# Blocks of two experts with four contraction rows instead of four experts with two, in a two-block transformer kernel on one Trainium2 core

## The chip, the core and the metric

The kernel runs on one core of a Trainium2 chip. A core has a matrix engine (PE, whose weight loads the profile lists apart as PEld), a vector engine (DVE), a scalar engine (ACT), a general engine (POOL) and an engine that here only issues transfers (SP). They run side by side, each through its own list of instructions in a fixed order, and wait for each other through semaphores. Weights come from the chip's memory (HBM) in transfers that 16 engines carry out. PE writes its results to PSUM, eight banks of 512 floats on each of 128 partitions; everything else is in SBUF. The metric is the time of one execution on the device, in microseconds (us).

## The reference

Two transformer blocks over 256 tokens of width 1024. The first mixes two kinds of attention and then sends each token to two of 32 experts; the second attends over the tokens and a context and has a plain gated MLP. The change lies in the first block's experts:

```python
def hierarchical_moe(h, w_group, w_router, w_gate, w_up, w_down):
    group_logits = jnp.einsum('td,dg->tg', h, w_group)      # top-1 of 4 groups
    ...
    top_p, top_i = lax.top_k(in_prob, EXPERT_TOPK)          # top-2 of its 8 experts
    ...
    for grp in range(N_GROUPS):
        hid = (jax.nn.silu(jnp.einsum('td,edf->tef', h, w_gate[grp]))
               * jnp.einsum('td,edf->tef', h, w_up[grp])) * combine[:, grp, :, None]
        y = y + jnp.einsum('tef,efd->td', hid, w_down[grp])
    return y
```

An expert's gate and up matrices are 1024 x 256, its down matrix 256 x 1024, all float32: 1 MB each, 96 MB for the 32 experts.

## The kernel before

The 32 experts are worked off in eight units of four (the loop over `u`). An expert has 32 places for tokens, so a unit has 128. For a unit, `gather(u)` makes the rows of its places, transposed, by products of x with one-hots (`pgat`, two groups of 16 instructions, each group followed by DVE's `xg`). Gate and up products (`pgu`) put four experts side by side on four groups of 32 columns of PE, eight contraction steps k each. ACT takes the silu (`sg`), DVE multiplies by the other half, PE transposes (`pth`), ACT copies (`hid`). The down products (`pyd`) fill two PSUM banks, one for each half nh of the 1024 columns, in two contraction steps k2. Each half is copied as a high part by ACT (`yh`) and a low part by DVE (`yl`), and products with transposed one-hots (`pst`, `ST`) scatter both into four running sums (`acc`, two token tiles by two halves).

The weights come in blocks of 1 MB, `[128, 2048]` floats, twelve for a unit: four each of gate (`eg`), up (`eu`) and down (`ed`). `wexp` makes one with a single transfer, issued by SP in `load_block` (L164). The blocks rotate through 21 slots (14 from unit 4 on); SP waits for the slot's last reader, then issues. Gate and up contraction row d sits on partition p = d // 8 with k = d % 8, so a partition's eight rows of an expert are 8 KB in a row in memory. A quarter took two of the eight rows, for all four experts: runs of 2 KB. A down block took one of a partition's two rows and one half of its columns, for four experts: also 2 KB.

```python
src = src.rearrange("e (p k) c -> p e (k c)", k=8)[:, :, part * 512:part * 512 + 512]
```

Between units 3 and 4 lies a branch (L1200) for tokens beyond an expert's 32 places, which all engines take part in; with these inputs it is not entered. From unit 5 on, PE also works on the context of block 2: the transposes of the normed context (`pt`, from `cx`), the projections `ckap`, `ckbp`, `cvbp`, and the transposes of its heads (`pka`, `pqk`). In unit 7 the sums are added to `x` (L1344), scaled to `xf` (L1348) and squared by ACT (`jk`, L1350), for each half and token tile; the sums of squares (`ss`) and then the splits of block 2's first weights (`lkah`, `lkal`) stand behind that.

The order on each engine isn't the order of the code: a scheduler sets it when the kernel is built, from its own estimates, save for a few pairs fixed by `after`. So a change in one place can move instructions elsewhere. On PE the helper records all products at L99 and all transposes at L102.

Of the kernel before, what the change touches and what calls it, by code (L numbers as in the profile page):

```python
# [22 lines left out]
# columns of the shape-only constant array  # L23
C_ID, C_TRI = 0, 128
C_IO = 256                     # 1..32 along the free axis
C_DN = C_IO + 32               # 8..1
C_SP = C_DN + 8                # p % 32 + 1
C_BM = C_SP + 1                # [p, 4]: p // 32 == j
C_SL = C_BM + 4                # rows of a modulation chunk's partial sums: latent, context
C_LT = C_SL + 2                # [i, j] of 8 by 8: j < i  # L30
C_W = C_LT + 64
# columns of the one of block 2's attention
C_ROPE = 0                     # [p, 2 token tiles, cos 64 | signed sin 64]
C_CM = C_ROPE + 256            # [p, 64]: NEG where the column lies outside row 63 - p % 64's neighbourhood
C_J = C_CM + 64                # reversal of each half's 64 rows, times the root of the head's size
# [3 lines left out]
def constants():  # L39
    """arrays that depend on the shapes alone"""  # L40
# [31 lines left out]
    # [e, unit, slot]: e == 4 * unit + slot // 32  # L72
# [4 lines left out]
class Ordered:  # L77
    """the tensor engine; between start() and stop() it takes its instructions in the program's order"""
# [16 lines left out]
    def stop(self):  # L95
        self.on = False
# [9 lines left out]
def tile_kernel(ctx: ExitStack, tc: tile.TileContext, I, out, dbg=None):  # L106
# [9 lines left out]
    def open_stage(name, psum, base=False):  # L116
        """the pools of one stage; psum: banks per tag"""
# [14 lines left out]
    def open_part(name, psum):  # L132
        """pools of a part of the stage: SBUF for what only the part needs, and all of its PSUM"""
        st = ExitStack()
        S_["tmp"] = st.enter_context(tc.tile_pool(name="tmp_" + name, bufs=1, reuse_waits="tile"))
        S_["ps"] = st.enter_context(tc.tile_pool(name="ps_" + name, bufs=1, space=PSUM, reuse_waits="tile"))
        S_["banks"] = psum
        return st
# [17 lines left out]
    # ---------------------------------------------------------------- helpers  # L156
    def load_block(src, name, extra=None):
        """src: DRAM AP [128, a, b] with a * b = 2048; extra: a pool and its slots that the stage adds to the ring"""
# [8 lines left out]
    def cols(w, c0, n=256):  # L167
        """columns c0:c0+n of a [1024, *] matrix, contraction row d = p * 8 + k"""
        return w[:, c0:c0 + n].rearrange("(p k) c -> p k c", k=8)

    def rows(w, r0):
        """rows r0:r0+256 of a [*, 1024] matrix, contraction row k * 128 + p"""
# [28 lines left out]
    def after(ins, first):  # L201
        """ins behind first in their engine's order"""
# [6 lines left out]
    def bcast_dma(dst, src, n):  # L209
        """n elements of DRAM copied to all partitions"""  # L210
        SP.dma_start(dst, bass.AP(tensor=src.tensor, offset=src.offset, ap=[[0, P], [1, n]]))

    def rstd_of(ssq, n, mean, eps, name):
        """(ssq * mean + eps) ** -0.5 over [128, n]"""
# [6 lines left out]
    def row_ssq(src, name, col=None):  # L221
        """src [128, 2, 1024] -> sums of squares [128, 2]"""
# [9 lines left out]
    def row_rstd(src, name):  # L232
        """src [128, 2, 1024] -> rstd [128, 2]"""
        return rstd_of(row_ssq(src, name), 2, 1.0 / D, EPS, name)

    def diags(r, name):
        """diagonal matrices of the two columns of r [128, 2]"""
# [5 lines left out]
    def norm_rows(src, name):  # L243
        """the rows' rstd, a column for each token tile"""
# [3 lines left out]
    def pairs_T(src, dg, tags, by_pair=False):  # L248
        """four PSUM tiles of pairs of k, [128 d, 2, 256 t]: see scaled_T"""
# [10 lines left out]
    def scaled_T(src, dg, tags, by_pair=False):  # L260
        """yields k, PSUM [128 d, 256 t] of src[t, p * 8 + k], times r[t] where dg = diags(r);
        tags: the banks of the four pairs of k, each open until its pair was taken"""
# [3 lines left out]
    # -------------------------------------------------------------- constants  # L266
# [13 lines left out]
    cols_ = const.tile([P, 4, 8], F32)    # gains down the partitions: attn_norm, ffn_norm, norm1_g, norm2_g  # L280
    gA, gF, gN1, gN2 = (cols_[:, i] for i in range(4))
    lvl = ab([P, 5, 32], "lvl", "lvl", dt=BF16)     # masks of the doubling

    mqk = ring.tile([P, 2048], F32, tag="blk", name="mqk")
    POOL.memset(mqk[:, :P], 0.0)                 # takes its slot of the ring
# [21 lines left out]
    maskn = const.tile([P, P], BF16)      # [j, i]: NEG where j > i  # L307
    maskc = const.tile([P, P], BF16)      # [i, j]: NEG where j > i

    # ============================================================ block 1: norm  # L310
# [33 lines left out]
    PE.transpose(pm, tri, ident)          # [i, j]: j <= i  # L344
# [15 lines left out]
    # ------------------------------------------------- modulations of block 2  # L360
# [4 lines left out]
    DVE.tensor_tensor(sc2t, sc2t, c2t, op=ALU.mult)                         # silu  # L365
    sil = ep.tile([P, 8, 2, 16], F32, tag="sil", name="sil")
    POOL.tensor_copy(sil, bc(sc2t.rearrange("p a k -> p k a"), 16))
    mod = pers.tile([P, 6, 8, 2], F32, tag="mod", name="mod")     # [p, vector, k, latent / context], d = p * 8 + k
    w_mod = I["w_mod_2"][0]

    def mod_steps():
        """a vector's quarters by column groups: column 8 c + k of group j is d = (32 j + c) * 8 + k, and blocks of 32
        by 32, transposed, bring its two sides to mod's places"""
# [35 lines left out]
    # ------------------------------------------------------ GDN q, k, v with conv  # L409
    gT = {}  # L410

    def proj_T(c0, name, sink):
        """columns c0:c0+256 in two [128 ch, 256 t] PSUM tiles, each given to sink with its place; a step at a time"""
# [21 lines left out]
    def gdn_proj(kind, base):  # L435
        def conv(c, pp_):
# [11 lines left out]
            DVE.scalar_tensor_tensor(o, th, 1.0, a, op0=ALU.add, op1=ALU.mult)   # 2 * silu  # L448
# [17 lines left out]
    # ------------------------------------------------------------- gates  # L466
# [1361 lines left out]
```

## Time and profile before

| What | Value |
|---|---|
| median of 3 runs | 882.71 us (881.35 to 885.22) |
| profiled execution, span | 879.8 us |
| PE busy | 825.3 us, 94% of the span |
| DVE, ACT, POOL busy | 422.3, 296.3, 105.6 us |
| transfers | 200.18 MB, mean 228 GB/s |
| eg, eu, ed blocks | 32 each, 1024 KB, 14.1 us median from issue to landing |

The span runs from the first to the last instruction that the profiler saw; the time of a run also holds what lies before and after. The experts run from about 228 to 477 us of the span. Busy shares are means over stages with different limits, so the stretches below say more than the table. A row of a timeline merges neighbours of the same kind on an engine: start, length, engine, line, operation, result <- operands, shapes, count, and in brackets how long the engine had been idle before and what ended that.

### The profile page before, as it was taken

How to read it: one execution, taken by the hardware profiler on the slowest of the kernel's cores; microseconds unless marked ns; L12 is line 12 of the kernel's file. 1: busy time of each engine (PE TensorE's matmuls, PEld its weight loads, DVE VectorE, ACT ScalarE, POOL GpSimd, SP SyncE). 2: the span in 40 equal slices, each digit the busy share in tenths (PEclk: the TensorE clock that was granted, in tenths of full speed). 3: DMA queues.
4: the chain of work that ended last, by engine and by line, in shares of the span. 5: the costliest groups of instructions: out<-in, count | busy, mean ns of one | idle time of the engine just before them, and what ended most of it. 6: DMA issues, size and time to landing. Idle time of an engine off the chain costs nothing.

```text
span 879.8 us, 15327 instructions
## 1 busy us (share of the span) xinstructions
PE 825.3 (94%) x6436; PEld 667.5 (76%) x6436; DVE 422.3 (48%) x927; ACT 296.3 (34%) x523; POOL 105.6 (12%) x90
## 2 busy tenths in 40 slices
PE   9999999999789988996998997999997999999997
PEld 8887887867656645773865897667686999999996
DVE  4866454644322111323224788555664655545555
ACT  4542143433110000101004662456643444444332
POOL 3111000332000000000000577100022100000000
PEclk9999999999889999897999999589999999999999
DMA  7999787495799999999599135010271655555101
GB/s 218 353 386 391 264 296 281 133 385 171 280 386 386 387 387 387 378 382 376 208 386 333 48 53 164 1 48 2 96 239 48 202 187 187 192 191 187 54 1 48
DMA packets 123416, 200.18 MB, mean 228 GB/s; under 512 B 15481, under 2 KB 62001, under 8 KB 123345
## 3 DMA queue, kind: packets, MB, share of 16 engines
q1 hardware_dynamic: 123152, 199.08, 64.5%
q8 instruction: 51, 0.84, 0.4%
q0 software_dynamic: 192, 0.11, 0.1%
q14 instruction: 21, 0.16, 0.1%
HBM read 198.23 MB, written 1.05 MB: 226 GB/s over the span
## 4 chain that ended last, share of the span: by engine, by line
PE 47%; DVE 4%; POOL 4%; issue 3%; DMA 2%; ACT 1%; SPq 1%; DVEq 0%; POOLq 0%; ACTq 0%
PE pfg L99 7%; PE pfu L99 7%; PE pf L99 7%; PE sc L99 6%; PE pgat L99 3%; PE pgu L99 2%; PE po L99 2%; PE ptp L102 2%; POOL latl L192 2%; PE pyd L99 2%; DMA eg<-in_w_gate_dram 1%; PE ckbp L99 1%; PE pqa L99 1%; PE pqb L99 1%; POOL rq L218 1%
## 5 line engine op out<-in xcount | busy, mean ns | idle before, releaser
L99 PEld LDWEIGHTS pgat<-S,x 128*128 128x128 f32 x256 | 62.5, 335 | 3.7 <-DVE xg L1051 2.1
L99 PE MATMUL pgat<-S,x 128*128 128x128 f32 x256 | 63.0, 404 | 0.6 <-PEq L1200 0.5
L99 PE MATMUL pfu<-lof,fuh 128*128 128x256 f32 x176 | 50.2, 285 | 0.0
L99 PE MATMUL pfu<-hif,fuh 128*128 128x256 f32 x176 | 50.2, 285 | 0.0
L99 PE MATMUL pfu<-hif,ful 128*128 128x256 f32 x176 | 50.2, 285 | 0.0
L99 PE MATMUL pfg<-hif,fgl 128*128 128x256 f32 x160 | 45.3, 283 | 0.0
L99 PE MATMUL pfg<-lof,fgh 128*128 128x256 f32 x160 | 45.2, 283 | 0.0
L99 PE MATMUL pfg<-hif,fgh 128*128 128x256 f32 x160 | 45.2, 283 | 0.0
L192 DVE TENSOR_TENSOR fdl<-fd,fdh 128x512 fp32r<-128x512 f32 x44 | 27.5, 687 | 31.0 <-ACT fdh L185 31.0
L1051 DVE TENSOR_TENSOR xg<-pgat,cols__83 128x512 f32<-128x512 f32 x15 | 10.4, 692 | 63.7 <-PE pgat L99 63.7
L99 PE MATMUL pyd<-ed,hid 128*32 128x512 f32 x256 | 34.1, 664 | 3.8 <-ACT hid L1326 3.8
L1320 ACT ACTIVATE sg<-pgu,r1s 128x256 f32<-128x256 f32 x8 | 3.8, 474 | 96.7 <-PE pgu L99 73.9
L1545 DVE TENSOR_REDUCE st<-sc 128x1 f32<-128x512 f32 x32 | 21.9, 691 | 28.6 <-PE sc L99 28.3
L185 ACT ACTIVATE fdh<-fd 128x1024 fp32r<-128x1024 f32 x22 | 22.1, 1052 | 39.0 <-issue 39.0
L99 PE MATMUL pf<-fdl,fh 128*128 128x512 f32 x88 | 35.0, 398 | 0.0
L99 PE MATMUL pf<-fdh,fh 128*128 128x512 f32 x88 | 34.7, 394 | 0.0
L99 PE MATMUL pf<-fdh,fl 128*128 128x512 f32 x88 | 34.1, 393 | 0.0
L99 PEld LDWEIGHTS pfu<-hif,fuh 128*128 128x128 f32 x176 | 34.1, 194 | 0.0
L99 PEld LDWEIGHTS pfu<-hif,ful 128*128 128x128 f32 x176 | 34.1, 193 | 0.0
L99 PEld LDWEIGHTS pfu<-lof,fuh 128*128 128x128 f32 x176 | 34.0, 193 | 0.0
L185 ACT ACTIVATE fuh<-fu 128x1024 fp32r<-128x1024 f32 x22 | 22.1, 1052 | 31.2 <-issue 28.7
L99 PE MATMUL sc<-k,qa 128*128 128x256 f32 (+1 forms) x64 | 28.1, 501 | 3.7 <-DVE qa L1149 3.5
(691 smaller groups left out, 2209.6 us busy)
## 6 DMA issues: line engine op xcount, KB each, us to landing
eg<-in_w_gate_dram SPq DMA_DIRECT2D x32, 1024.0 KB, 14.1
eu<-in_w_up_dram SPq DMA_DIRECT2D x32, 1024.0 KB, 14.1
ed<-in_w_down_dram SPq DMA_DIRECT2D x32, 1024.0 KB, 14.1
wmod<-in_w_mod_dram SPq DMA_DIRECT2D x24, 1024.0 KB, 9.5
fg<-in_w_gate_dram SPq DMA_DIRECT2D x11, 1024.0 KB, 5.4
fu<-in_w_up_dram SPq DMA_DIRECT2D x11, 1024.0 KB, 5.3
fd<-in_w_down_dram SPq DMA_DIRECT2D x11, 1024.0 KB, 5.0
kv<-in_w_in_dram SPq DMA_DIRECT2D x5, 1024.0 KB, 13.9
```

Source lines behind the costliest of these rows:

```text
L99: return self._keep(self.engine.matmul(*args, **kwargs))
L102: return self._keep(self.engine.transpose(*args, **kwargs))
L185: S_["hi"] = ACT.activation(hf[:, s], vf[:, s], AF.Copy)
L192: i = (POOL if c in pool else DVE).tensor_tensor(lf[:, s], vf[:, s], hf[:, s], op=ALU.subtract)
L218: S_["pow"] = POOL.tensor_tensor(r, v, mhalf[:, :n], op=ALU.pow)
L1051: DVE.tensor_tensor(xg[:, ks], p, bc(gF[:, ks], P), op=ALU.mult)
L1320: ACT.activation(sg, pgu[:, 0], AF.Silu, scale=r1s[:, u:u + 1])
L1545: DVE.tensor_reduce(t_[:, 0, s_:s_ + 1], sc, axis=AX.XY, op=ALU.max)
```

## The change

A block now holds two experts instead of four, and for each a run of 4 KB: four of a partition's eight gate or up rows, or a whole row of the down matrix. `part % 2` chooses the pair of experts, `part // 2` the half of the contraction rows. Each step k of a gate or up product thus reads two blocks (j = 0, 1 from one, j = 2, 3 from the other). Since a down block now has all columns of one contraction row, the loop over k2 goes outside that over the halves, both banks are open at once, and both copies come behind all 32 instructions. The line that kept unit 7's second half behind the scatter of the first is gone.

```diff
-        src = w[u // 2, 4 * (u % 2):4 * (u % 2) + 4]
-        if name == "ed":
-            src = src.rearrange("e (p k) c -> p e k c", k=2)[:, :, part % 2, part // 2 * 512:part // 2 * 512 + 512]
-        else:
-            src = src.rearrange("e (p k) c -> p e (k c)", k=8)[:, :, part * 512:part * 512 + 512]
-        return load_block(src, name, extra)
+        e0 = 4 * (u % 2) + 2 * (part % 2)
+        src = w[u // 2, e0:e0 + 2].rearrange("e (p k) c -> p e (k c)", p=P)
+        return load_block(src[:, :, part // 2 * 1024:part // 2 * 1024 + 1024], name, extra)
...
-                                     rhs=ww[k // 2][:, j, k % 2 * 256:k % 2 * 256 + 256], start=k == 0, stop=k == 7)
+                                     rhs=ww[k // 4 * 2 + j // 2][:, j % 2, k % 4 * 256:k % 4 * 256 + 256], start=k == 0, stop=k == 7)
...
-        for nh in range(2):
-            py = pt_([P, 512], ("y", "y" if u < IFU else "cx")[nh], "pyd")
-            for k2 in range(2):
+        pys = [pt_([P, 512], t, "pyd") for t in ("y", "y" if u < IFU else "cx")]
+        for k2 in range(2):
+            for nh, py in enumerate(pys):
                 for j in range(4):
-                    m = PE.matmul(py[32 * j:32 * j + 32], lhsT=hid[:, k2, 32 * j:32 * j + 32],
-                                  rhs=dw[2 * nh + k2][:, j], start=k2 == 0, stop=k2 == 1)
-                    if u == 7 and nh and j + k2 == 0:
-                        after(m, S_["sc"])
+                    PE.matmul(py[32 * j:32 * j + 32], lhsT=hid[:, k2, 32 * j:32 * j + 32],
+                              rhs=dw[2 * k2 + j // 2][:, j % 2, nh * 512:nh * 512 + 512], start=k2 == 0, stop=k2 == 1)
+        for nh, py in enumerate(pys):
             yh = c2.tile([P, 512], F32R, tag="y", name="yh", bufs=NY)
```

The order of the transfers on SP stays as it was, and so does that on POOL. Units 0 to 2 keep their order on PE. What moves on PE, in unit 3 behind the transposes of the hidden rows (acc_2743 and acc_2745 are the sums of the first half of the columns, acc_2744 and acc_2746 those of the second; an order row of `pyd` or `pgu` counts one for two instructions of the trace):

```order
-L99 MATMUL pyd<-ed,hid 32x512 x8
+L99 MATMUL pyd<-ed,hid 32x512 x16
 L99 MATMUL acc_2743<-yh,ST 128x512
 L99 MATMUL acc_2745<-yh,ST 128x512
-L99 MATMUL pyd<-ed,hid 32x512 x4
+L99 MATMUL acc_2744<-yh,ST 128x512
+L99 MATMUL acc_2746<-yh,ST 128x512
 L99 MATMUL acc_2743<-yl,ST 128x512
 L99 MATMUL acc_2745<-yl,ST 128x512
-L99 MATMUL pyd<-ed,hid 32x512 x4
-L99 MATMUL acc_2744<-yh,ST 128x512
-L99 MATMUL acc_2746<-yh,ST 128x512
```

The down products were cut in three with the first half's scatter between them; now they stand in one row, with all scatter products behind.

PE in unit 4, from the scatter on (pgat is the gather for unit 5, in two groups):

```order
+L99 MATMUL acc_2744<-yh,ST 128x512
+L99 MATMUL acc_2746<-yh,ST 128x512
 L99 MATMUL acc_2743<-yl,ST 128x512
 L99 MATMUL acc_2745<-yl,ST 128x512
 L99 MATMUL pgat<-S,x 128x128 x8
-L99 MATMUL pyd<-ed,hid 32x512 x4
-L99 MATMUL pgat<-S,x 128x128 x8
-L99 MATMUL acc_2744<-yh,ST 128x512
-L99 MATMUL acc_2746<-yh,ST 128x512
 L99 MATMUL acc_2744<-yl,ST 128x512
 L99 MATMUL acc_2746<-yl,ST 128x512
+L99 MATMUL pgat<-S,x 128x128 x8
```

Between the two groups of the gather stood the last quarter of the down products; now one pair of scatter products stands there. Unit 6 moves in the same way. In unit 5, behind the context's projection `ckbp`, 16 rows of up products stand instead of 8, and 8 fewer ahead of it.

DVE at the end of unit 7, before:

```order
L1338 TENSOR_TENSOR yl<-pyd,yh 128x512
L1344 TENSOR_TENSOR x<-x,acc_2743 128x512
L1344 TENSOR_TENSOR x<-x,acc_2745 128x512
L1348 TENSOR_TENSOR xf<-x,fB 128x512 x2
L1338 TENSOR_TENSOR yl<-pyd,yh 128x512
L1344 TENSOR_TENSOR x<-x,acc_2744 128x512
L1344 TENSOR_TENSOR x<-x,acc_2746 128x512
```

And the same place now (the lines of the code are four fewer):

```order
L1334 TENSOR_TENSOR yl<-pyd,yh 128x512 x2
L1340 TENSOR_TENSOR x<-x,acc_2743 128x512
L1340 TENSOR_TENSOR x<-x,acc_2745 128x512
L1340 TENSOR_TENSOR x<-x,acc_2744 128x512
L1340 TENSOR_TENSOR x<-x,acc_2746 128x512
L1344 TENSOR_TENSOR xf<-x,fB 128x512 x4
```

All four additions now stand ahead of the first scaling. ACT's eight squarings keep their order, x and xf in turn.

## Rows read from the trace of the kernel before

**Rows 1.** Stretches: length, busy us (count) by engine, clock, transfer share, GB/s

```profile
80.00:88.00 8.00, 7.89 (x74) 7.07 (x72) 4.33 (x13) 1.45 (x2) 3.01 (x4) 1.00 1.03 410
...
287.00:309.40 22.40, 20.82 (x204) 14.43 (x203) 3.73 (x6) 2.05 (x4) 0.00 (x0) 1.00 1.05 386
...
400.00:410.00 10.00, 5.91 (x29) 1.41 (x27) 2.93 (x6) 2.35 (x4) 0.00 (x0) 0.53 1.05 369
```

**Rows 2.** Timeline of SP, the loads of block 2's modulation

```profile
70.53 25.07 SPq L164 DMA_DIRECT2D wmod<-in_w_mod_dram  x6
```

**Rows 3.** Waits of PE, 225 to 490 us: us in total, times, longest

```profile
PE pth L102 <- DVE sg L1321: 7.3, 6, 1.9
...
PE pth L102 <- DMA eg<-in_w_gate_dram: 0.6, 1, 0.6
...
PE pgc L102 <- DVE gcol L1280: 0.3, 1, 0.3
PE pst L99 <- DVE gcol L1280: 0.2, 1, 0.2
```

**Rows 4.** Timeline of PE and ACT, down products of units 2 and 3

```profile
296.15 3.64 PE L99 MATMUL pyd<-ed,hid 128*32 128x512 f32 x32 [0.47 <-ACT hid L1326]
...
299.86 0.60 ACT L1337 ACTIVATE yh<-pyd 128x512 fp32r<-128x512 f32 x1 [1.06 <-PE pyd L99]
...
318.61 1.92 PE L99 MATMUL pyd<-ed,hid 128*32 128x512 f32 x16 [0.47 <-ACT hid L1326]
...
326.08 0.73 PE L99 MATMUL acc<-yl,ST 128*128 128x512 f32 x2
```

**Rows 5.** Timeline, unit 4's last up products and its silu

```profile
343.59 3.66 PE L99 MATMUL pgu<-eu,xg 128*32 128x256 f32 x64
...
348.07 0.47 ACT L1320 ACTIVATE sg<-pgu,r1s 128x256 f32<-128x256 f32 x1 [22.77 <-SPq L1200]
```

**Rows 6.** Timeline of PE and DVE, the gathers in units 4 and 6

```profile
350.15 2.78 PE L99 MATMUL pyd<-ed,hid 128*32 128x512 f32 x24 [0.53 <-ACT hid L1326]
...
354.15 3.85 PE L99 MATMUL pgat<-S,x 128*128 128x128 f32 x16
...
358.93 4.10 PE L99 MATMUL pgat<-S,x 128*128 128x128 f32 x16
...
366.96 4.18 PE L99 MATMUL pt<-dgc,cx 128*128 128x128 f32 x16 [1.14 <-issue]
...
445.79 3.64 PE L99 MATMUL pyd<-ed,hid 128*32 128x512 f32 x32 [0.47 <-ACT hid L1326]
...
454.49 0.69 DVE L1051 TENSOR_TENSOR xg<-pgat,cols__83 128x512 f32<-128x512 f32 x1 [3.42 <-PE pgat L99]
...
454.76 0.62 PE L99 MATMUL acc<-yl,ST 128*128 128x512 f32 x2
455.24 4.10 PE L99 MATMUL pgat<-S,x 128*128 128x128 f32 x16
```

**Rows 7.** Timeline of PE, unit 5 around the context's heads

```profile
395.02 1.07 PE L99 MATMUL pgu<-eu,xg 128*32 128x256 f32 x16
399.23 1.09 PE L102 MATMUL pqk<-cst,qn__3722 128*128 128x128 f32 x4 [3.14 <-DVE qn__3722 L1089]
...
405.50 4.69 PE L99 MATMUL pyd<-ed,hid 128*32 128x512 f32 x24 [0.47 <-ACT hid L1326]
```

**Rows 8.** Timeline of PE, DVE and ACT, end of unit 7

```profile
468.47 1.92 PE L99 MATMUL pyd<-ed,hid 128*32 128x512 f32 x16 [0.47 <-ACT hid L1326]
...
472.38 1.29 DVE L1344 TENSOR_TENSOR x<-x,acc 128x512 f32<-128x512 f32 x2 [0.59 <-PE acc L99]
...
474.36 0.63 ACT L1350 ACTIVATE jk<-xf 128x512 bf16<-128x512 f32 x1 [0.54 <-DVE xf L1348]
...
479.62 0.63 ACT L1350 ACTIVATE jk<-x 128x512 bf16<-128x512 f32 x1
...
480.37 0.63 ACT L1350 ACTIVATE jk<-xf 128x512 bf16<-128x512 f32 x1
```

More of the change, by code (lines that the diff above doesn't have):

```diff
@@ L1340, in tile_kernel @@
                 PE.matmul(acc[2 * tt + nh], lhsT=ST[:, tt * P:(tt + 1) * P], rhs=yh, start=u == 0, stop=False)
-                S_["sc"] = PE.matmul(acc[2 * tt + nh], lhsT=ST[:, tt * P:(tt + 1) * P], rhs=yl, start=False, stop=u == 7)
+                PE.matmul(acc[2 * tt + nh], lhsT=ST[:, tt * P:(tt + 1) * P], rhs=yl, start=False, stop=u == 7)
                 if u == 7:
```

## Prediction

> **What bounds the kernel now.** I read the trace in this order: busy time by stretch, the waits of PE, then the timelines of the places where the change moves something.
>
> By stretch first. While the experts run, the transfer engines are full: from 287 to 309 us they move 386 GB/s at a share of 1.05 [rows 1]. One block of 1,048,576 bytes takes 2.72 us at that rate. If this set the pace, longer runs would be the thing to want. PE, however, is busy 20.82 of the 22.40 us of that stretch [rows 1], and the list of what PE waited for between 225 and 490 us has one row with a transfer in it, 0.6 us [rows 3]; even there the same place also hangs on the heads of the context. PE's larger waits are short handovers to DVE and ACT: 7.3 us in six pieces before the transposes of the hidden rows [rows 3]. So the blocks arrive ahead of their use, and the stage is PE's instruction stream plus the handovers in it. A faster load is worth something only where somebody waits for its landing.
>
> There is one such place. In unit 4 PE's last up product ends at 347.25 (343.59 + 3.66), but ACT's silu starts at 348.07, and what released it is SP behind the branch on overflow [rows 5]. SP leaves that branch when the loads that it had issued have landed, so this release hangs on the transfers.
>
> **The change part by part.**
>
> *The loads.* As many blocks, as many bytes, half as many runs, twice as long. The trace of before holds runs of 4 KB: a wmod block is two rows of 1024 floats. Six of them are issued one behind the other from 70.53 [rows 2], and from 80 to 88 us the engines move 410 GB/s [rows 1]: 2.56 us a block, 0.16 less. Ends: 0 (runs make no difference) and 0.16; I take 0.16, since nothing but the run length tells those blocks from the experts'. Units 2 to 4 are 36 blocks of a full queue ahead of the branch: SP's release comes about 5.8 us earlier, near 342.
>
> The Trainium skill, "DMA: Bandwidth & Descriptors", section Specifications, puts the smallest transfer for line rate at 512 B, so by it 2 KB runs lose nothing and 4 KB runs gain nothing. The rows disagree: 386 against 410 GB/s [rows 1]. What the kernel would do if the page were right is the second rival.
>
> *Gate and up products.* As many, of the same shape; each k now needs two blocks, so a unit's second block is wanted some 0.9 us earlier (a quarter of the 3.66 that 64 instructions take [rows 5]), and its first is given back as much later. PE waits for no block now [rows 3], and the transfer queue is full [rows 1]; costed at nothing. If the cover is gone, it costs those 0.9 us a unit.
>
> *Down products.* The 32 of a unit now stand in one row, and both copies (ACT's yh, DVE's yl) come behind it. In unit 2 they already stood so: 32 take 3.64 us, and the second copy starts 3.71 after the first product (299.86 - 296.15) [rows 4]. The copy takes 0.60, then come four pairs of scatter products; a pair takes 0.5 (454.76 to 455.24) [rows 6]. With T0 the first down product, the order yh, yh, yl, yl gives: second yh at T0 + 4.4, first yl at 4.9, next thing at 5.4.
>
> Unit 3: before, the last pair started at 326.08, which is T0 + 7.47 [rows 4], since each half's scatter waited for its copy by itself. After: T0 + 5.4. Gain 2.1. Unit 4's up products then end earlier by that and by the two waits on gcol, 0.3 and 0.2 [rows 3], whose transposes now stand apart: 347.25 becomes 344.65, SP's release (342) is past, and the silu starts at 344.7 instead of 348.07. **Term A: -3.4.** If the loads don't get faster, SP still holds ACT until 348 and A is nothing.
>
> Unit 4: before, the first gather stood between the two halves and the last quarter of the down products, and the second gather began at 358.93, T0 + 8.78 [rows 6]. After: gather one at T0 + 5.4, 3.85 long (354.15), and the second needs the same PSUM bank, so it waits for DVE's xg: the last product to the second gather is 0.79 (xg at 454.49, gather at 455.24, from unit 6) [rows 6]. T0 + 10.04. The rest of the old filling work is gone from this hole. What is late next is the chain behind xg on DVE (one-hots, squares of cx, dgc) and with it the transposes of the context at 366.96, for which PE already waits 1.14 [rows 6]. **Term B: +1.3.** Unit 6 has the same hole: before T0 + 9.45 (455.24 - 445.79), after T0 + 5.6 + 3.85 + 0.79. **Term D: +0.8.** In unit 5 the four pcw products stand between and give the copy time: 0 to 0.8, taken +0.3 (**C**).
>
> Unit 5, heads of the context: before, the last 8 rows of up products (16 instructions, 1.07 us at 395.02) stood behind ckbp; now 16 rows do. The projection ends some 0.9 earlier, its norm runs on ACT, DVE and POOL under PE's work, and the transposes pqk, for which PE waited 3.14 at 399.23 [rows 7], come 0.9 earlier. **Term E: -0.9.**
>
> Unit 7: before, the first half's sums were added, scaled and squared while PE made the second half. First addition at 472.38, T0 + 3.91; first squaring of xf at 474.36, 1.98 later; last squaring at 480.37 [rows 8]. Now the first addition comes at T0 + 5.45 (+1.55), and four additions stand ahead of the first scaling instead of two, 1.29 for two as timed, 1.2 from start to start. First squaring of xf: 474.36 + 2.75 = 477.1; six more behind it at 0.75 (479.62 to 480.37) [rows 8]: last at 481.6. **Term F: +1.2**, since the splits of block 2's first weights stand behind the squarings on ACT. PE itself ends earlier there, which nobody waits for.
>
> *Downstream.* The order in block 2's attention also moves: transposes ptp go behind outputs po, DVE's st operations change places. As much work, on a PE that has few holes there. Ends -1.5 and +1.5 from nothing but the short handovers seen elsewhere [rows 3]; taken 0.
>
> **Sum:** -3.4 + 1.3 + 0.3 + 0.8 - 0.9 + 1.2 = -0.7 against the profiled span of 879.8: 879.1. The median of the runs, 882.71, lies 2.9 over that span; I take that as what lies around it. **Forecast 882.0**, no change that can be measured (about 0.5%, 4.4 us, is what this kernel's timing can tell).
>
> **The rivals.**
>
> *The loads set the pace after all.* 72 blocks are loaded at a full queue from unit 2 on; 72 x 0.16 = 11.5 us, 871.2. For it: a share of 1.05 [rows 1]. Against: no row of PE's waits [rows 3]. 0.06.
>
> *The rate stays* (the blocks go out in 2 KB pieces anyway, or run length doesn't matter: the change doesn't do what it says). SP holds the silu of unit 4 as before, A is 0, the other terms stay: +2.7, 885.4. Against: 410 GB/s. By the page on DMA it is this one. 0.12.
>
> *Slower, by the clock.* Between 400 and 410 us PE was granted 0.53, mostly its lower level of 1.2 GHz, after the wait of 3.14 for pqk; 24 down products at 405.50 took 4.69 us [rows 1, 7], where 32 took 3.64 at 2.4 GHz [rows 4]. So 10 us at the lower level hold 5.8 us of work and cost 4.2. The change widens PE's hole ahead of the context's transposes (1.14 to 2.4) and shifts everything behind it. If two more such stretches follow, +8.4: 890.4. It decides once 12 us more than now run at 1.2 GHz. 0.13.
>
> *Faster, by the clock.* The same with the other sign: the hole ahead of pqk shrinks, the stretch at 400 goes: -4.2, 877.8, more if block 2 gains a stretch too. 0.13.
>
> **How the numbers follow.** Forecast 0.56, its terms uncertain by some 2.5 us together. Faster by over 0.5% (under 878.3): the first rival and most of the last, 0.16. Slower (over 887.1): most of the clock's 0.13 and the tails of the forecast and the second rival, 0.15. Within: 0.69. Range 877 to 888: outside are the first rival, and the far halves of the two clocks, 0.18.
>
> **What would show it.** Between 264 and 309 us near 410 GB/s, not 386. In unit 4 the silu released by PE, not SP, 3 us earlier. In unit 3 one wait of PE between down products and scatter, and the unit 2 us shorter. A wait of over 2 us ahead of the context's transposes; pqk's wait near 2.3; in unit 7 the last squaring 1.2 later after the first down product. I am wrong if PE shows waits for transfers, if units 0 to 2, where I put nothing, get shorter or longer, or if the stretches at 1.2 GHz change by more than 6 us.

## Result: 0.98% slower, and the profile after

| | before | after |
|---|---|---|
| median of 7 runs | 882.63 us (881.35 to 885.22) | 890.95 us (884.83 to 896.86) |
| span of the profiled execution | 879.8 us | 888.2 us (its time 889.98) |
| PE busy | 825.3 us | 835.8 us |
| transfers, packets | 200.18 MB, 123,416 | 200.18 MB, 98,839 |

The ratio is 1.0098, with a 95% interval of 1.0072 to 1.0125: 8.3 us slower, outside the predicted range of 877 to 888. DVE and ACT were as busy as before (422.3 and 296.3 us). PE did the same products in 10.5 us more. The ratios here and below are close to ratios of means, and runs over 1.5% above their kernel's fastest don't count in them (four in experiment 7, one each in 9 and 14).

The blocks did get faster. The stretches of the changed kernel that answer to [rows 1]:

```profile
80.00:88.00 8.00, 7.89 (x75) 7.09 (x73) 4.33 (x13) 1.57 (x2) 3.00 (x4) 1.00 1.03 410
288.70:311.10 22.40, 20.81 (x204) 14.40 (x203) 3.62 (x6) 2.05 (x4) 0.00 (x0) 1.00 1.02 408
401.00:411.00 10.00, 7.65 (x37) 2.64 (x39) 2.38 (x7) 0.38 (x1) 0.00 (x0) 0.66 0.62 195
```

The expert loads move 408 GB/s instead of 386, and PE is busy 20.81 us of the stretch as it was 20.82. The Trainium skill, "DMA: Bandwidth & Descriptors", section Specifications, puts line rate at 512 B and more; between runs of 2 and 4 KB the trace still shows that difference.

The lag of the changed trace behind the one of before tells where the time went. At unit 0's first gate product it is 1.47 us (237.33 against 235.87), at the first split of the latent's projection in block 2 it is 6.18 (ACT, `lath`, 504.47 against 498.29), at block 2's output projection 9.39, in the MLP 8.39. So, of the 8.4 us of the profiled run, 1.5 lie ahead of the experts, the experts cost 4.7, block 2's attention 3.2, and 1.0 came back behind it. The first 1.47 arose before any expert ran: this trace has 1.2 GHz at 175.7 to 179.1. The eighth experiment, which runs the experts of before, shows the same stretch and a lag of 1.48 at that place, so it doesn't belong to the change.

What the experts did, by unit. The down products, whole kernel, in the page of before and then of after (busy us and mean ns of one, behind the bar):

```profile
L99 PE MATMUL pyd<-ed,hid 128*32 128x512 f32 x256 | 34.1, 664 | 3.8 <-ACT hid L1326 3.8
```

```profile
L99 PE MATMUL pyd<-ed,hid 128*32 128x512 f32 x256 | 38.2, 662 | 3.8 <-ACT hid L1323 3.8
```

As many, each as long, 4.1 us more of PE's time in all: fewer of them ran at once. Timeline of PE, units 3, 5, 6 and 7 of after, to lay beside [rows 4, 6 to 8]:

```profile
320.42 3.67 PE L99 MATMUL pyd<-ed,hid 128*32 128x512 f32 x32 [0.47 <-ACT hid L1323]
...
404.44 5.29 PE L99 MATMUL pyd<-ed,hid 128*32 128x512 f32 x24 [0.47 <-ACT hid L1323]
409.66 1.06 PE L99 MATMUL pcw<-combr,S 128*128 128x6 f32 x8
410.64 1.91 PE L99 MATMUL pyd<-ed,hid 128*32 128x512 f32 x8
...
446.48 3.63 PE L99 MATMUL pyd<-ed,hid 128*32 128x512 f32 x24 [0.47 <-ACT hid L1323]
450.04 0.28 PE L99 MATMUL pst<-rrT,esel 32*128 32x256 bf16 x1
450.25 1.91 PE L99 MATMUL pyd<-ed,hid 128*32 128x512 f32 x8
...
471.80 4.97 PE L99 MATMUL pyd<-ed,hid 128*32 128x512 f32 x32 [0.47 <-ACT hid L1323]
```

Unit 3 takes the 3.67 us that were predicted. In unit 6 the 32 instructions take 3.63 + 1.91 instead of 3.64, in unit 7 4.97. Three stretches of equal length inside unit 6's row, down products alone (columns: length, PE busy and count, weight loads, DVE, ACT, clock, transfer share, GB/s), show why:

```profile
446.40:448.15 1.75, 1.67 (x16) 0.53 (x18) 0.00 (x0) 0.00 (x0) 1.00 1.03 412
448.15:449.90 1.75, 1.75 (x12) 0.35 (x6) 0.00 (x0) 0.00 (x0) 1.00 1.03 410
450.20:451.95 1.75, 1.70 (x8) 0.38 (x8) 0.00 (x0) 0.60 (x1) 1.00 0.99 391
```

In 1.75 us PE starts 16 of them at first and 8 at the end, at full clock. The built kernel tells what stands there. Written out by expert, bank a for the first half and b for the second, unit 6's row is:

```
a0 a1 a2 a3  b0 b1 b2 b3  a0 a1  b0 b1  pst  a2 a3  b2 b3
```

The products of one half's step now need two blocks, and the scheduler put those of the pair of experts in the earlier block ahead of the other pair's, and `pst`, a product over all 128 columns, between the pairs. Behind the first eight, each pair has only itself to run beside: `b0 b1` need the columns of `a0 a1`, the other two experts stand behind `pst`, and there `b2 b3` need the columns of `a2 a3`. Two abreast take the time of four. The Trainium skill, "TensorEngine Tiling (Array Packing)", section Key Properties, says that tiles work independently of each other and that a change of the tiling mode drains the engine. The 16 starts of the first stretch agree with the first part; the drain can't be told apart from the cut here. In units 3 and 4 the same order by pairs has nothing in between, and the pairs of neighbouring steps overlap: 3.67 us.

### The profile page after: what moved, and what is told of

It is laid out like the page before. It is cut to its first block, busy times and chain, and to the rows that moved or that the text cites. A ratio compares the mean times of both kernels' runs of the same rounds, so it can differ in the third digit from the quotient of the medians.

```text
span 888.2 us, 15321 instructions
## 1 busy us (share of the span) xinstructions
PE 835.8 (94%) x6436; PEld 674.6 (76%) x6436; DVE 422.3 (48%) x927; ACT 296.3 (33%) x523; POOL 105.2 (12%) x90
## 2 busy tenths in 40 slices
DMA packets 98839, 200.18 MB, mean 225 GB/s; under 512 B 15480, under 2 KB 62000, under 8 KB 98768
## 4 chain that ended last, share of the span: by engine, by line
PE 49%; DVE 5%; POOL 4%; issue 3%; ACT 1%; DMA 1%; DVEq 0%; SPq 0%; POOLq 0%; ACTq 0%
PE pfg L99 7%; PE pfu L99 7%; PE pf L99 7%; PE sc L99 6%; PE pgat L99 4%; PE pgu L99 3%; PE pyd L99 2%; PE po L99 2%; PE ptp L102 2%; POOL latl L192 2%; PE ckbp L99 2%; POOL rq L218 1%; PE pqa L99 1%; PE pqb L99 1%; DMA cst<-in_cst_dram 1%
## 5 line engine op out<-in xcount | busy, mean ns | idle before, releaser
L99 PE MATMUL pyd<-ed,hid 128*32 128x512 f32 x256 | 38.2, 662 | 3.8 <-ACT hid L1323 3.8
L99 PE MATMUL sc<-k,qa 128*128 128x256 f32 x64 | 30.6, 533 | 3.7 <-DVE qa L1146 3.5
```

What stands on the lines that cost most here:

```text
L99: return self._keep(self.engine.matmul(*args, **kwargs))
```

## The experiments

Each ran 12 times beside before on the same chip, if nothing else is said. A kernel's runs spread mostly by the clock of block 2, so beside median and ratio (95% interval) I give the fastest run and the number of *far* runs, those 6.5 us or more over that kernel's own fastest. The changed kernel has 3 far runs of 7; before has 9 of 148 in all. "Lag out of the experts" is the profiled run's lag behind before at `lath` less that at unit 0's first gate product: +4.7 for the changed kernel. Profiled runs of kernels with the same experts differ in it: the changed kernel's give 4.7, 4.6 (experiment 3) and 5.9 (11), experiment 1's give -1.2 and +0.2 (9). So 1.4 is its noise.

**1. Four abreast** (what is undone: the rows' order)

```diff
+        PE.start()
         for k2 in range(2):
...
+        PE.stop()
...
+                if g > 2:
+                    after(m, S_["dn"])
...
+        if u > 5:
+            after(m, S_["dn"])
```

Between `start` and `stop` PE keeps the order of the code; the two `after` put `pcw` and `pst` behind the row.

> The changed kernel with the 16 down products of a unit held in one row, the four experts of a group always side by side, and the small products that stood inside the rows of units 5 and 6 put behind them; blocks, loads and the order of block 2's attention on PE stay. Theory 'two abreast': in units 5 and 6 the row is cut by a product over the whole array, and behind the cut the experts go two at a time, so that the row takes 5.1 us from first to last start in unit 6 instead of 3.05. Then the row of unit 6 comes back to about 3.05, that of unit 5 shortens by about 1.7, unit 7 stays as it is because its last block lands late: 3.4 us less than the changed kernel, about 887.5. Rival 'it is all block 2 and the clock': the rows shorten but the time stays within 1 us of the changed kernel, 890 to 892.

882.67 us, 1.0008 (0.9973 to 1.0044): the median is back by 8.3 us, 4.9 more than expected. Fastest run 877.64 against 884.83 of the changed kernel; far runs 5 of 12, so the median lies just under a gap (882.81 to 887.84), and the fastest run, 7.2 us better, says more. PE in units 6 and 7:

```profile
442.71 3.64 PE L99 MATMUL pyd<-ed,hid 128*32 128x512 f32 x32 [0.47 <-ACT hid L1327]
446.29 0.28 PE L99 MATMUL pst<-rrT,esel 32*128 32x256 bf16 x1
446.50 0.73 PE L99 MATMUL acc<-yh,ST 128*128 128x512 f32 x2
...
465.43 2.77 PE L99 MATMUL pyd<-ed,hid 128*32 128x512 f32 x20 [0.47 <-ACT hid L1327]
468.38 1.91 PE L99 MATMUL pyd<-ed,hid 128*32 128x512 f32 x12 [0.18 <-DMA ed<-in_w_down_dram]
```

Unit 6's row is whole again; unit 7's still isn't, and PE waits there for a down block. The lag out of the experts is -1.2, 5.9 better than the changed kernel, where the two rows explain 3.4. The order by pairs had also finished bank a just ahead of b: in unit 4 the first copy started 3.79 us after the row (352.49 - 348.70), here 2.91 (350.45 - 347.54), and the gather behind it came that much earlier.

**2. Old blocks, new row**

```diff
-                              rhs=dw[2 * k2 + j // 2][:, j % 2, nh * 512:nh * 512 + 512], ...
+                              rhs=dw[2 * nh + k2][:, j], ...
```

with `wexp` and the gate products as before.

> The blocks of before (four experts, two rows, runs of 2 KB) with the changed kernel's down products (both halves' products first, then both copies); PE's order in block 2's attention comes out as in the changed kernel. Theory 'two abreast': no row is cut into twos here, since each product group needs one block; unit 3 keeps only part of its 2.1 us, the silu of unit 4 is released by SP again near 348, and the terms B and F of the prediction stay: about 885 if block 2's order costs nothing, 887.5 if it costs the 2 us by which the changed kernel's trace falls back between 573 and 700 us. Rival 'the order of the down products is the loss': 890 or more, with rows of 3.05 to 5 us in units 5 to 7 but the same total. Rival 'the blocks are the loss': 882.6, as before.

881.86 us, 1.0016 (0.9983 to 1.0049); fastest 880.26, far 4 of 12, lag out of the experts +1.3. The third theory's number, but the edit reached less than it says. As built, both halves' products alternate in units 0 to 2, 5 and 6 alone. In units 3 and 4 the scheduler kept the order of before, and in unit 7 it put scatter products ahead of the last four. Unit 3:

```profile
319.56 1.92 PE L99 MATMUL pyd<-ed,hid 128*32 128x512 f32 x16 [0.47 <-ACT hid L1326]
322.20 0.73 PE L99 MATMUL acc<-yh,ST 128*128 128x512 f32 x2 [0.72 <-ACT yh L1336]
322.87 1.06 PE L99 MATMUL pyd<-ed,hid 128*32 128x512 f32 x8
323.86 0.73 PE L99 MATMUL acc<-yl,ST 128*128 128x512 f32 x2
324.52 1.06 PE L99 MATMUL pyd<-ed,hid 128*32 128x512 f32 x8
```

So it shows that the alternating order of units 5 and 6 costs nothing in the median while no group of four is parted; it says nothing on the row of units 3 and 4. With old blocks a group of four needs one block, and none was parted.

**3 and 4. Block 2's order swapped**

```diff
+            for a, b in zip(row, row[1:]):
+                after(b, a)
```

where `row` holds PE's, DVE's or ACT's instructions of the attention, sorted by a table.

> The changed kernel, with the instructions of PE, DVE and ACT in block 2's attention held in the order that they have in the kernel before (a table of numbers). Theory 'order': in the changed kernel's trace the lag grows from 6.2 to 9.4 us between 573 and 602 us, where this order differs and PE runs at 1.2 GHz for 37.5 us instead of 27.3; with the old order 2 to 3 us come back: 888 to 889, and the stretch at 1.2 GHz from about 555 us is some 27 us long. Rival 'the clock by itself': the stretch differs from run to run whatever the order, and the median stays at 890 to 892.

> The kernel before, with PE, DVE and ACT in block 2's attention held in the order that they have in the changed kernel; blocks and experts as before. Theory 'order': 2 to 3 us slower than before, 885 to 885.5, with a stretch at 1.2 GHz from about 549 us that is some 37 us long instead of 27. Rival 'the clock by itself': within 1 us of before, 882 to 883.5.

891.63 us, 1.0095 (1.0062 to 1.0127), for the changed kernel with the old order; 880.45 us, 0.9975 (0.9949 to 1.0000), far 1 of 12, for before with the new one. The order falls as a cause: it brings nothing back and costs nothing. The third run's profile has even more of the lower clock. The stretches 577 to 592 and 592 to 609 us, of before's twin (experiment 13) and then of this run:

```profile
577.00:592.00 15.00, 15.00 (x99) 10.45 (x98) 9.46 (x27) 8.92 (x24) 0.00 (x0) 1.00 0.08 19
592.00:609.00 17.00, 16.81 (x118) 12.54 (x116) 8.27 (x21) 8.33 (x18) 0.00 (x0) 1.00 0.12 47
```

```profile
577.00:592.00 15.00, 15.00 (x66) 10.25 (x66) 5.42 (x13) 6.04 (x14) 0.00 (x0) 0.50 0.00 0
592.00:609.00 17.00, 17.00 (x76) 11.41 (x76) 7.30 (x23) 7.21 (x19) 0.00 (x0) 0.60 0.18 63
```

PE has hardly a hole in either; at a granted clock of 0.50 and 0.60 it gets through 142 products where 217 went.

**5. Twos in old blocks** (the cut alone, put into experiment 2)

```diff
+        if u in (5, 6):
+            row[8:] = [(1, nh, 2 * h + j) for h in range(2) for nh in range(2) for j in range(2)]
...
+            after(m, S_["cut"][0])
+            after(S_["cut"][1], m)
```

> The second experiment's kernel (blocks of before, both halves' down products in one row) with one difference: in units 5 and 6 the row is cut where the changed kernel's is, 12 products, then the small product over the whole array, then 4 products, the experts behind the first half going two at a time. Nothing of the loads or of block 2 differs. Theory 'two abreast': the row of unit 6 takes 5.1 us from first to last start instead of 3.05, unit 5's grows likewise, and the first half's copy, which can start only when the twos are through, comes later too: 4 to 5 us slower than the second experiment's 881.9, so 886 to 887. Rival 'it is the long blocks, not the order in the row': within 1 us of 881.9.

889.51 us, 1.0070 (1.0028 to 1.0111); fastest 884.13, 3.9 over experiment 2's; lag out of the experts +5.4, 4.1 over it. Unit 6:

```profile
448.63 3.63 PE L99 MATMUL pyd<-ed,hid 128*32 128x512 f32 x24 [0.47 <-ACT hid L1332]
452.19 0.28 PE L99 MATMUL pst<-rrT,esel 32*128 32x256 bf16 x1
452.39 1.91 PE L99 MATMUL pyd<-ed,hid 128*32 128x512 f32 x8
```

With runs of 2 KB and nothing else changed, the cut costs what theory said, and both traces have as much of the lower clock between the two marks (30.7 us); the median went further (7.7), and 6 of 12 runs are far against 4.

**6. Gate and up blocks alone**

```diff
+            e0 = 2 * (part % 2)
+            src = src[e0:e0 + 2].rearrange("e (p k) c -> p e (k c)", p=P)[:, :, part // 2 * 1024:part // 2 * 1024 + 1024]
```

> Gate and up blocks of two experts with four rows (runs of 4 KB); down blocks, down products and their order as in the kernel before, so no row is cut into twos. Theory: the faster loads are worth only what hung on a transfer, the 0.8 us by which SP held the silu of unit 4 (347.25 to 348.07 in the trace of before): 881.5 to 882.5. Rival 'a block that is freed later lands later': unit 7's last down block comes after its use and PE waits for it, 0.5 to 1 us more than before, 883 to 884.

883.24 us, 1.0006 (0.9975 to 1.0036), far 1 of 12, lag out of the experts -0.3. That is 0.7 over the expected range. Two thirds of the loads are faster, and all that hung on them was the 0.8 of unit 4's silu (the lag of unit 4's down products less unit 3's is -0.8). The rival's late block isn't there: no wait of PE for a transfer, though SP issues unit 7's last down blocks 1.96 us behind the first gate product, as in the changed kernel.

**7. Unit 7 as before** (added to experiment 1)

```diff
+        if name == "ed" and u == 7:
+            src = w[u // 2, 4 * (u % 2):4 * (u % 2) + 4].rearrange("e (p k) c -> p e k c", k=2)
```

> The first experiment's kernel (four experts abreast in every row) with unit 7's down blocks and down products as in the kernel before: four experts with two rows, the first half's products and scatter ahead of the second half's. Its last block is then wanted some 4 us later in the unit. Theory 'the last block lands late': PE's wait for a transfer in unit 7 goes (the row lost 1.2 us in the first experiment's trace), and the squarings ahead of block 2 get their 1.2 us back: 2 to 2.5 us less than the first experiment's 882.7, 880 to 881. Rival 'block 2 hides it': the trace's lag behind before at 498 us (first split of the latent's projection) stays at -1.2 and the time stays at 882 to 883.

889.84 us, 1.0014 (0.9971 to 1.0057; the medians stand at 1.008): fastest 878.83, but far 7 of 12. In the trace it did what was expected, lag out of the experts -3.2 (2.0 better than experiment 1, with 3.4 us less at the lower clock in it); the median missed by the far runs, which experiments 13 to 17 go after.

**8 to 11. Idle products ahead of the attention**, in before, experiment 1, experiment 7 and the changed kernel

```diff
+    for i in range(15):
+        S_["fill"] = PE.matmul(pw, lhsT=ident, rhs=ident, start=True, stop=True)
```

> The kernel before with 15 products of 128x128 that nobody reads, in PE's idle 3.5 us ahead of block 2's attention (546.1 to 549.8 in its trace); PE's order there is free otherwise. Theory 'the hole brings the lower clock': the stretch at 1.2 GHz from 549 to 577 us goes, which costs 0.42 us for each of its us by unit 5's down products: up to 11 us less, 872 to 876, and the runs lie closer together. Rival 'the lower clock comes from what PE does in the attention': a stretch of 20 us or more at 1.2 GHz stays, and the time is within 2 us of 882.5.

> The first experiment's kernel (four experts abreast in every row) with the eighth's 15 idle products ahead of block 2's attention. In that place the runs of a kernel lay closer together (877 to 884 in the eighth experiment, 878 to 890 in the first). Theory 'the experts' part is what counts': its trace entered block 2 1.2 us ahead of before, so about 1.2 us under the eighth experiment's 882.5: 881, with all runs under 886. Rival 'the clock of block 2 decides': runs of 888 to 890 stay, half of them.

> The seventh experiment's kernel (four abreast, unit 7 as before) with the 15 idle products. Its trace entered block 2 2.9 us ahead of before. Theory 'the experts' part is what counts': 879 to 880, faster than both kernels. Rival 'the clock of block 2 decides': two groups again, 879 to 881 and 889 to 892, as in the seventh experiment.

> The changed kernel with the 15 idle products and nothing else. Theory 'rows by twos and a late block': the lag that the changed kernel brings out of the experts, 4.7 us without what its trace had lost before they began (6.2 less 1.5), is there whatever the clock does later: 4 to 5.5 us over the eighth experiment's 882.5, 886.5 to 888. Rival 'the loss sits in block 2's clock, which the idle products change': within 2 us of 882.5.

Before with them: 882.45 us, 0.9976 (0.9950 to 1.0003), far 2 of 12, in two groups, 877.0 to 879.4 (five runs) and 882.4 to 884.1. In the profiled run (883.45) the hole is filled, and the lower clock comes all the same:

```profile
546.00:551.00 5.00, 5.00 (x46) 5.00 (x45) 4.97 (x6) 0.00 (x0) 5.00 (x6) 1.00 0.07 26
551.00:586.00 35.00, 34.68 (x127) 22.76 (x125) 19.34 (x50) 16.33 (x43) 2.90 (x3) 0.56 0.00 1
```

so the hole alone isn't what brings it. Experiment 1 with them: 880.73, 0.9992 (0.9961 to 1.0023), far 4 of 11, against the expectation of none; a twelfth run took 1124.09 us at a mean clock of 0.642 and isn't counted. Experiment 7 with them: 879.28, 0.9951 (0.9934 to 0.9968), no far run of 6, as expected. The changed kernel with them (6 runs): 891.63, 1.0080 (1.0050 to 1.0110), far 3, lag out of the experts +5.9: over the 886.5 to 888 expected, and the loss stays, whatever stands ahead of the attention.

**12. No last block** (experiment 1 without the load of unit 7's last down block; its products read the third, so that part of the result is left out; one run)

```diff
+        first[u] = [[wexp(w, u, q, nm) for q in range(3 if u == 7 and nm == "ed" else 4)] for w, nm in ((wg_, "eg"), (wu_, "eu"), (wd_, "ed"))]
```

> The first experiment's kernel without the load of unit 7's last down block: its products read the third block instead (that part of the result is left out; as many products as before). Theory 'the last block lands late': the row of unit 7 takes 3.05 us from first to last start instead of 4.27, with no wait for a transfer in it, and the first split of block 2 comes 1.2 us earlier after the row's start. Rival 'the second bank or the scatter products hold the row': it stays at 4.2 or more.

```profile
467.27 3.64 PE L99 MATMUL pyd<-ed,hid 128*32 128x512 f32 x32 [0.47 <-ACT hid L1327]
```

The run took 879.64 us. The row is whole, and from its start to `lath` it is 30.4 us instead of 31.6. The late block costs 1.2.

**13 to 15. The one row in some units** (old blocks; `ROWS` is units 0 to 4, then 5 and 6, then 7)

```diff
+        if u in ROWS:
+            for k2 in range(2):
+                for nh in range(2):
+                    down(k2, nh)
```

> Blocks of before; both halves' down products in one row in units 0 to 4 alone. All else is as before, block 2's order too. If the lower clock of many runs came with the row in these units, 4 or more of 12 runs lie over 887 us; otherwise the median is 882.5 within 1 us and at most 1 or 2 runs lie there.

> Blocks of before; both halves' down products in one row in units 5 and 6 alone. If the lower clock of many runs came with these units' rows, 4 or more of 12 runs lie over 887 us; otherwise 882.5 to 883.5 (unit 6's second gather waits up to 0.8 us longer) and at most 1 or 2 runs there.

> Blocks of before; both halves' down products in one row in unit 7 alone. Theory: the row of unit 7 moves the squarings ahead of block 2 (term F, 1.2 us) and with them the phase in which block 2 meets the clock: 4 or more of 12 runs over 887 us, median 882 to 884. Rival: unit 7 has no part in it, at most 1 or 2 runs over 887.

Units 0 to 4: 882.71 us, 1.0000 (0.9987 to 1.0013), far 0. Units 5 and 6: 885.02, 1.0047 (1.0014 to 1.0081), far 5 of 12, all at 894 to 897. Unit 7: 881.06, 0.9978 (0.9964 to 0.9991), far 0. But the three edits reached less, and more, than they say. As built, the first changes only units 0 to 2, with units 3 and 4 as before, and no mark of its trace is 0.3 us from before's. The third leaves unit 7's row in halves and moves only the scatter. The second does alternate the halves in units 5 and 6, but its attention comes out in an order on PE, DVE and ACT that is neither before's (experiment 13) nor the changed kernel's (15). So the far runs go with the row in units 5 and 6 or with that order. In its profiled run, a far one, PE is at the lower clock already in unit 4, where it runs what before runs at full clock:

```profile
350.90:357.80 6.90, 6.22 (x27) 1.54 (x28) 0.78 (x2) 0.98 (x2) 0.00 (x0) 0.51 1.05 365
```

This doesn't settle it either: experiments 9 and 12 show 3.4 us of the lower clock near that place, in runs that aren't far.

**16. Long blocks, each half by itself, four abreast**

```diff
         for nh in range(2):
             py = pt_([P, 512], ("y", "y" if u < IFU else "cx")[nh], "pyd")
+            PE.on, PE.last = True, PE.last if nh else None
```

> The changed kernel's blocks, four experts abreast, each half's down products and copies by themselves as in the kernel before (the two halves' products one behind the other in units 3 to 6), small products behind the rows. The first half's copies can start 1.7 us after the row instead of 2.9, so units 3 and 4 gain 2 to 3 us on before; unit 7's last block is wanted 0.9 us earlier than in the first experiment, so PE waits about 2 us for it. Theory 'the lower clock goes with the one row': 880 to 882 and at most 1 or 2 of 12 runs 6.5 us over the fastest. Rival 'it goes with the long blocks': the same 880 in the fastest runs, but 4 or more of 12 runs 6.5 us over them.

886.31 us (8 runs), 1.0045 (1.0027 to 1.0064), lag out of the experts -1.4, far 0, but all runs at a clock of 0.947 to 0.955, and a stretch of 41.0 us at 1.2 GHz in block 2: a miss by 4 to 6 us in the level, and neither theory has it. Unit 7's first half shows the late block once more, as a plain wait:

```profile
465.47 1.91 PE L99 MATMUL pyd<-ed,hid 128*32 128x512 f32 x12 [0.47 <-ACT hid L1327]
468.30 1.05 PE L99 MATMUL pyd<-ed,hid 128*32 128x512 f32 x4 [0.92 <-DMA ed<-in_w_down_dram]
```

**17 and 18. The row to unit 4 only** (experiment 7 with down blocks and products of units 5 and 6 as before too; then with the idle products)

```diff
-        if name == "ed" and u == 7:
+        if name == "ed" and u >= 5:
```

> Gate and up blocks of the changed kernel in all units, its down blocks and its one row of down products, four experts abreast, in units 0 to 4; down blocks and products of units 5 to 7 as in the kernel before. Theory 'the row in units 5 and 6 brings the lower clock of many runs': at most 1 or 2 of 12 runs lie 6.5 us over the fastest (7 of 12 in the seventh experiment), and the median is that kernel's faster group, 879 to 881, under before. Rival 'the long blocks bring it': 4 or more of 12 runs there and a median of 885 to 890.

> The same with 15 idle products in PE's idle 3.5 us ahead of block 2's attention, as in the eighth and tenth experiment. Expected 877 to 879.5, 0.4 to 0.6% under before, without runs over 884. Rival: as without them, 879 to 881.

880.67 us, 0.9966 (0.9942 to 0.9989), far 0 of 12, all runs between 879.2 and 881.7: faster than both kernels, if only by 0.3%. With the idle products 882.18, 0.9982 (0.9946 to 1.0018), far 1 of 12: no help, the rival's number or worse.

## Why the prediction was wrong

**The step that failed is the down products.** The prediction said that the 32 of a unit "now stand in one row", took 3.64 us for them from unit 2 [rows 4], and built the terms C, D and F on it. In units 5 and 6 the row was cut, and two experts ran where four had run: 7.20 and 5.54 us instead of 5.75 and 3.64. The order by names shows a row of 12, small products and a row of 4 there, but not which experts; I read it as a row, and the section on the change, which has unit 6 move as unit 4 does, leaves `pst` out. Experiments 1 and 5 show the cause from both sides: undone, together with the order by pairs in all units, it gives the fastest run 7.2 us and the median 8.3; put alone into another kernel, it costs the fastest run 3.9 and the median 7.7.

**"Costed at nothing", the gate products' blocks.** The condition that the prediction named came true in unit 7: the cover was gone. SP issues unit 7's last two down blocks as gate blocks come free:

```profile
464.53 0.88 SPq L164 DMA_DIRECT2D ed<-in_w_down_dram  x2
467.98 0.55 SPq L164 DMA_DIRECT2D kv<-in_w_in_dram  x1
```

464.53 is 1.96 us behind the unit's first gate product (462.57); before it was 1.13 (460.40 - 459.27). That alone costs nothing (experiment 6). But the last block is now wanted earlier too: with the pairs side by side its products could start in the middle of the row, 1.7 us behind its start, where before they came 4.9 behind it. Price by experiment 12: 1.2 us in unit 7, against the 0.9 a unit named. PE's list of waits for 225 to 490 us doesn't show it, since the experts of the other block still ran; in experiments 1 and 16 it shows.

**The terms themselves** held as far as they can be told apart. Lag after each step: A, -3.3 (from 1.81 to -1.45 from unit 3's to unit 4's down products), predicted -3.4, with PE instead of SP releasing the silu:

```profile
346.61 0.47 ACT L1317 ACTIVATE sg<-pgu,r1s 128x256 f32<-128x256 f32 x1 [21.37 <-PE pgu L99]
```

B, +1.8 (the context's transposes at 367.29 against 366.96), predicted +1.3. E, -0.9, predicted -0.9, though a stretch at 1.2 GHz is 3.4 us shorter there, so the two can't be told apart. C, D and F stand mixed with the failed step: unit 5's row to unit 6's gate product +1.8, where the cut alone is 1.45 (5.29 + 1.91 against 4.69 + 1.06) and C was +0.3; unit 6's row to unit 7's gate product +2.6, the cut's 1.9 and 0.7 for D (predicted 0.8); unit 7's row to `lkah` +2.5, the late block's 1.3 and 1.1 for F (predicted 1.2). Three waits in the list of after (us in total, times, longest), the heads' and the context's as predicted, the last one that of units 3 and 4 between row and scatter:

```profile
PE pqk L102 <- DVE qn__3722 L1086: 2.3, 1, 2.3
...
PE pt L99 <- DVE dgc L240: 2.0, 1, 2.0
...
PE acc L99 <- ACT yh L1333: 1.5, 2, 0.8
```

Two cut rows, 1.45 and 1.9, and a late block of 1.3 make 4.65; with the predicted -0.7 that is +4.0, and +4.7 was measured, which agrees within the noise of 1.4. What lies around the span was 1.8 us (889.98 - 888.2), not 2.9, which decides nothing.

**Downstream, taken as 0 with ends of 1.5:** too narrow by far. Block 2's attention cost 3.2 in the profiled run, not by its order (experiments 3 and 4) but by its clock: 37.5 us at 1.2 GHz instead of 27.3. The two stretches, of before and then of after:

```profile
549.00:577.00 28.00, 27.04 (x83) 16.94 (x84) 15.24 (x40) 12.52 (x31) 3.27 (x3) 0.51 0.00 1
```

```profile
555.00:592.00 37.00, 35.84 (x122) 23.60 (x122) 19.22 (x48) 15.79 (x40) 3.48 (x3) 0.50 0.00 1
```

"Slower by the clock", the rival with 890.4 and a chance of 0.13, named the right number by luck, as over half of it was lost in the experts, and a part of the truth: 10.2 us more at 1.2 GHz in block 2. So one of the prediction's own signs of being wrong came true, more than 6 us of change at 1.2 GHz; no wait for a transfer is in the list, and units 0 to 2 took as long as before (73.9 us between the first gate products of units 0 and 3, 73.5 before). That rival's place and trigger were wrong: behind the wider hole ahead of the context's transposes PE was at 1.2 GHz for 3.4 us instead of 6.8, and filling the one ahead of the attention (experiment 8) didn't end it. The rival "the loads set the pace" is excluded by experiment 6, "the rate stays" by the 408 GB/s.

**What stays open.** Of the changed kernel's 8.3 us, the three traces with its experts show 4.6 to 5.9 lost there; the rest goes with the clock of block 2 and isn't explained. Over all batches 42 of 102 runs were far in kernels with both halves' row in units 5 and 6, 14 of 240 in the others, and taking that row and its down blocks out of experiment 7 took it from 7 of 12 to none, with block 2's attention in the same order on PE, DVE and ACT in both. Against it stand experiment 10, which has the row and no far run of 6, and experiment 16, which hasn't it and whose runs all lie at the lower clock without being far by the count. So the row goes with the far runs, but isn't shown to cause them. How an order 100 to 145 us ahead of the attention could decide how long PE stays at 1.2 GHz there, the runs don't show.

## What to carry to other kernels

Where several small products share PE by columns, a step is only as cheap as its full group: if operands of one group come in two blocks, a scheduler may part it, and a single product over all columns in the gap doubles the time of the parted step (a row of 5.54 us instead of 3.64), so fix the group's order by hand. Longer runs in memory are worth what somebody waits for; here they and the new order of unit 3 together gained 3.3 us up to one branch, where the loads alone (experiment 6) were worth 0.8, and 1.2 went back where a block came late. And where runs differ by the clock, compare the fastest runs and the lags at fixed marks before believing a median, and take the spread of those marks from kernels that are alike up to them. Read the order that was built, too: an edit may not reach the instructions that it names.

## What the runs showed of the hardware

Two products of 32 columns side by side take as long as four: 16 starts in 1.75 us against 8, at full clock. Runs of 4 KB load at 408 GB/s where runs of 2 KB gave 386. In block 2's attention PE, with hardly a hole, spent from 23.9 to 51.2 us at 1.2 GHz in the profiled runs, and the time from `lath` to the output projection followed: -1.9 us at 23.9, 0 at 27.3, +3.2 at 37.5, +9.7 at 51.2, about 0.4 for each. It rose or fell without a change in order (27.3 in before against 51.2 in experiment 3), and 15 idle products ahead of it didn't prevent it. In block 1, where nothing was changed, six of the profiled runs show 3.4 us at 1.2 GHz near 175.7, the others near 11 us or not at all; the first kind is 1.5 us late at unit 0.
